# A one-row copy from ScalarE beside each group of a row softmax

## The chip, the cores and the metric

The kernel runs on one core of a Trainium2 chip. The core has five engines with an instruction stream each: TensorE (not used here), VectorE (DVE in the profile), ScalarE (ACT), GpSimd (POOL) and SyncE (SP, which issues DMA transfers). The metric is the device time of one execution in microseconds, lower is better. A profile is taken of one execution; its span runs from the first to the last instruction.

## The reference

A softmax over the last dimension of a float32 tensor with 16,384 rows of 512 elements (33.55 MB in, 33.55 MB out):

```python
batch, seq, dim = 16, 1024, 512
def reference(x):
    x_max = np.max(x, axis=-1, keepdims=True)
    exp_x = np.exp(x - x_max)
    return (exp_x / np.sum(exp_x, axis=-1, keepdims=True)).astype(np.float32)
```

## The kernel before

The 16,384 rows are cut into 16 groups. A group is 8 rows on each of the 128 partitions, a tile of 128 x 4096 float32 (2 MB). All tiles lie in `ring`, a buffer in on-chip memory with room for 12 groups; a group is worked on in place.

Transfers move two groups at a time, 4 MB: loads L0 to L7 (line 127) and stores S0 to S7 (line 131). Both are issued by SyncE, in a fixed order. The first six loads fill the ring at the start, the very first ahead of the opening barrier. After that SyncE follows `ORDER`, written out by hand: S0 S1 L6 L7 S2 S3 S4 S5 S6 S7. Before a store it waits until both groups are scaled (line 170), before L6 and L7 until S0 and S1 have landed, since these loads reuse the ring (line 197). At the end it waits for all stores (line 199).

Per group, three steps:

1. Row maxima, negated, on VectorE (`rowmax`, line 145), for one group ("M") or two ("MM") in an instruction. It waits for the load and counts up the semaphore `maxima`.
2. Exponentials on ScalarE (`exps`, lines 149 to 155): a hardware loop over the 16 groups. Each turn waits for `maxima`, computes the group's place in the ring, and issues 8 activations (line 134), one for each of the partition's rows, 128 x 512, with the negated maximum as bias and the row's sum accumulated into `stat`. The eighth counts up `summed`.
3. Scaling (`scale`, lines 157 to 163): VectorE waits for `summed`, takes the reciprocal of the 8 sums (line 159), and then VectorE ("D") or GpSimd ("P") multiplies the group by it (line 161) and counts up the semaphore that the store waits for.

VectorE's order is written out in `SEQUENCE`: M0 M1 M2 D0 M3 D1 MM4 P2 MM6 D3 P4 MM8 D5 P6 MM10 D7 P8 MM12 D9 P10 MM14 D11 P12 D13 D14 D15. It does its instructions strictly in that order, so a reciprocal that waits for ScalarE also holds up the row maxima behind it. ScalarE issues no transfers.

Of the kernel before, what the change touches and what calls it, by code (L numbers as in the profile page):

```python
# [15 lines left out]
GROUP = 8  # L16
# [44 lines left out]
def kernel(  # L61
# [5 lines left out]
    nc = tc.nc  # L67
# [3 lines left out]
    x_rows, out_rows = x.flatten_outer_dims(), out.flatten_outer_dims()  # L71
# [11 lines left out]
    def sem(name):  # L83
        return ctx.enter_context(nc.semaphore(name))

    maxima, summed, inverted = [sem(s) for s in ("maxima", "summed", "inverted")]
    loaded = [sem(f"loaded{k}") for k in range(len(LOADS))]
    scaled = [sem(f"scaled{k}") for k in range(len(STORES))]

# [43 lines left out]
    def exp(row, one):  # L133
        return nc.scalar.activation(  # L134
            out=row, in_=row, func=EXP, bias=one, scale=1.0, accum_out=one
        )
# [5 lines left out]
    def rowmax(g, groups):  # L142
# [3 lines left out]
            out=cols(stat, g, groups), in_=rows(g, groups), axis=AX, negate=True  # L146
        ).then_inc(maxima, groups)

    def exps():
        with nc.Fori(0, GROUPS, 1, engines=(ACT,)) as g:  # L150
            nc.scalar.wait_ge(maxima, 1).then_inc(maxima, -1)  # L151
            row = nc.scalar.snap((g % RING) * GROUP)
            for r in range(GROUP):
                done = exp(ring[:, bass.ds((row + r) * d, d)], stat[:, bass.ds(row + r, 1)])
            done.then_inc(summed, 1)

# [23 lines left out]

    nc.scalar.preload_act_table(EXP)  # L181
    exps()
    for work in SEQUENCE.split():
        kind = work.rstrip("0123456789")
# [46 lines left out]
```

## Time and profile before

| what | value |
|---|---|
| time, median of 3 runs | 159.97 us (159.87 to 160.02) |
| the profiled execution | 160.08 us, of which span 158.8 us |
| DVE busy | 121.8 us (77%) |
| ACT busy | 92.2 us (58%) |
| POOL busy | 42.3 us (27%) |
| line 134, an activation of 128 x 512 | 707 ns, 128 of them |
| line 145, row maxima of one group / of two | 4415 ns / 8650 ns |
| line 161, multiply on DVE / on POOL | 5109 ns / 7016 ns |
| transfers | 8 loads and 8 stores of 4096 KB |
| issue to landing, median | loads 25.9 us, stores 24.0 us |

Busy time counts an engine's work, not its waits, nor the issuing of transfers. "DMA share" is the part of the time in which the core's 16 DMA engines have packets under way. A transfer is told by its issue on the queue of the issuing engine (SPq for SyncE) and by its landing, the moment its semaphore is complete. In a list by time the columns are start, duration, engine, line, operation, output and input, and in brackets the idle time before it and what ended that. In the rows of an issue the three numbers of ns are the shortest, median and longest duration of the issuing instruction, then come the first and the last start in us.

### The profile page before, as it was taken

The page shows a single profiled execution, that of the slowest core. Times are in us where ns is not written, and L with a number is a line of the kernel's source. Part 1 is how long each engine was busy: PE and PEld are TensorE (multiplying, and loading weights), DVE is VectorE, ACT ScalarE, POOL GpSimd, SP SyncE. Part 2 cuts the span into 40 slices and gives each one's busy share as a digit, 9 for nine tenths or more (in the row PEclk, how much of TensorE's full clock was granted, in tenths as well). Part 3 has the DMA queues.
Part 4 walks back from the last instruction along what each step waited for, and adds up shares of the span by engine and source line. Part 5 has one row for each costly group of instructions (what it writes and reads, how often), then busy time and mean ns, then how long its engine had stood idle before and what let it go on. Part 6 is the DMA issues. An engine that isn't in the chain of part 4 may idle for free.

```text
span 158.8 us, 572 instructions
## 1 busy us (share of the span) xinstructions
DVE 121.8 (77%) x36; ACT 92.2 (58%) x257; POOL 42.3 (27%) x10
## 2 busy tenths in 40 slices
DVE  0008979999999999999999499999999999700000
ACT  0300699969406999999988990899599300000000
POOL 0000000000007903930970790079049300000000
DMA  7999999999999999999999999999999999999996
GB/s 264 438 479 405 405 495 421 396 438 471 413 405 438 471 405 396 396 413 471 438 396 462 446 413 405 454 421 438 438 421 446 413 446 438 438 421 438 429 429 264
DMA packets 2304, 67.11 MB, mean 423 GB/s; under 512 B 256, under 2 KB 256, under 8 KB 256
## 3 DMA queue, kind: packets, MB, share of 16 engines
q1 hardware_dynamic: 2304, 67.11, 98.9%
HBM read 33.55 MB, written 33.55 MB: 423 GB/s over the span
## 4 chain that ended last, share of the span: by engine, by line
DMA 45%; DVE 39%; issue 2%; DVEq 0%
DMA ring<-in_x_dram 26%; DVE ring L161 22%; DMA out_dram<-ring 20%; DVE stat L145 16%; DVE recip L159 1%; DVEq L144 0%
## 5 line engine op out<-in xcount | busy, mean ns | idle before, releaser
L134 ACT ACTIVATE ring<-ring,stat x128 | 90.4, 707 | 28.1 <-ACTq L151 28.1
L145 DVE TENSOR_REDUCE stat<-ring 128x16 f32<-128x8192 f32 (+1 forms) x10 | 69.5, 6956 | 15.7 <-DMA ring<-in_x_dram 15.7
L161 POOL TENSOR_TENSOR ring<-ring,recip 128x4096 f32<-128x4096 f32 x6 | 42.1, 7016 | 81.8 <-DVE recip L159 81.8
L161 DVE TENSOR_TENSOR ring<-ring,recip 128x4096 f32<-128x4096 f32 x10 | 51.1, 5109 | 0.3
L134 ACT ACTIVATION_READ_ACCUMULATOR ring<-ring,stat x128 | 23.8, 186 | 0.0
L181 ACT ACT_TABLE_LOAD x1 | 1.3, 1283 | 4.0 <-PEq L179 4.0
L159 DVE RECIPROCAL recip<-stat 128x8 f32<-128x8 f32 x16 | 3.0, 190 | 0.0
L215 POOL MEMSET const-float32-0.0<- 128x1 f32 x1 | 0.1, 98 | 0.2 <-issue 0.2
L215 POOL MEMSET const-bfloat16-1.0<- 128x1 bf16 x1 | 0.1, 102 | 0.0
L215 POOL MEMSET const-uint8-127<- 128x1 uint8 x1 | 0.1, 102 | 0.0
L215 POOL MEMSET const-float32-1.0<- 128x1 f32 x1 | 0.1, 98 | 0.0
## 6 DMA issues: line engine op xcount, KB each, us to landing
ring<-in_x_dram SPq DMA_DIRECT2D x8, 4096.0 KB, 25.9
out_dram<-ring SPq DMA_DIRECT2D x8, 4096.0 KB, 24.0
```

Of the source, the lines that this page charges most:

```text
L134: return nc.scalar.activation(out=row, in_=row, func=EXP, bias=one, scale=1.0, accum_out=one)
L145: nc.vector.reduce_max(out=cols(stat, g, groups), in_=rows(g, groups), axis=AX, negate=True).then_inc(maxima, groups)
L159: nc.vector.reciprocal(out=cols(recip, g), in_=cols(stat, g)).then_inc(inverted, 1)
L161: engine.tensor_mul(out=rows(g), in0=rows(g), in1=spread(cols(recip, g))).then_inc(scaled[store_of(g)], 1)
L181: nc.scalar.preload_act_table(EXP)
L215: nc = _bacc.Bacc("TRN2", target_bir_lowering=False, num_devices=1)
```

## The change

At the start of every turn of ScalarE's loop, after the wait for `maxima`, ScalarE issues a transfer of its own: row 0 of `x` (512 float32, 2 KB) is copied in main memory to the last row of the output. Ahead of the eighth activation of the turn ScalarE waits until the copy has landed, and takes the semaphore back to zero. The last store, S7, writes the same output row after all copies have landed, since it waits for group 15, whose eighth activation waits for the last copy.

```diff
     maxima, summed, inverted = [sem(s) for s in ("maxima", "summed", "inverted")]
+    copied = sem("copied")
...
     def exps():
         with nc.Fori(0, GROUPS, 1, engines=(ACT,)) as g:
             nc.scalar.wait_ge(maxima, 1).then_inc(maxima, -1)
             row = nc.scalar.snap((g % RING) * GROUP)
+            nc.scalar.dma_start(out=out_rows[-1:, :], in_=x_rows[:1, :]).then_inc(copied, 16)
             for r in range(GROUP):
+                if r == GROUP - 1:
+                    nc.scalar.wait_ge(copied, 16).then_inc(copied, -16)
                 done = exp(ring[:, bass.ds((row + r) * d, d)], stat[:, bass.ds(row + r, 1)])
             done.then_inc(summed, 1)
```

## The prediction

> **What bounds the kernel now.** I read the page's counts of DMA first, then the chain of waits, then the DMA issues one by one, then the order of time on ScalarE and VectorE. The page says:
>
> ```profile
> span 158.8 us, 572 instructions
> DMA  7999999999999999999999999999999999999996
> DMA packets 2304, 67.11 MB, mean 423 GB/s; under 512 B 256, under 2 KB 256, under 8 KB 256
> q1 hardware_dynamic: 2304, 67.11, 98.9%
> DMA 45%; DVE 39%; issue 2%; DVEq 0%
> ```
>
> One queue, q1, carries everything, and its packets fill 98.9% of sixteen engines' span. 256 packets are small (16 transfers on 16 engines: their completions), the other 2048 carry 67.11 MB, 32 KB each. The chain's share of 39% for DVE is no bound: it runs through VectorE because a store was issued there, but stores queue. The issues show this; for the first loads, the last of the six early loads (the largest number of its line), and stores S0, S6 and S7:
>
> ```profile
> L127 SPq DMA_DIRECT2D ring<-in_x_dram x2: 333/358/383, 0.0 to 0.8; - x2
> DMA to landing us min/median/max: 12.3/16.8/21.2
> ...
> L127 SPq DMA_DIRECT2D ring<-in_x_dram x3: 444/473/524, 1.6 to 2.7; - x3
> DMA to landing us min/median/max: 39.8/49.0/58.6
> ...
> L131 SPq DMA_DIRECT2D out_dram<-ring x1: 347/347/347, 40.0 to 40.0; - x1
> DMA to landing us min/median/max: 31.1/31.1/31.1
> ...
> L131 SPq DMA_DIRECT2D out_dram<-ring x1: 332/332/332, 128.7 to 128.7; - x1
> DMA to landing us min/median/max: 20.4/20.4/20.4
> ...
> L131 SPq DMA_DIRECT2D out_dram<-ring x1: 332/332/332, 137.8 to 137.8; - x1
> DMA to landing us min/median/max: 20.9/20.9/20.9
> ```
>
> The first load lands at 12.3 us, the last store at 137.8 + 20.9 = 158.7. That is 15 more transfers in 146.4 us, 9.76 us each. S6 lands at 128.7 + 20.4 = 149.1, S7 9.6 later: S7 was issued 11.3 us before its turn came. The first load took 12.3 - 9.76 = 2.5 us beyond its own moving time, so S7 had 11.3 - 2.5 = 8.8 us to spare. S0 was issued at 40.0 while loads were queued until 2.7 + 58.6 = 61.3. The bound is therefore the DMA stream, and computation has slack. How much ScalarE has, its first group shows:
>
> ```profile
> 17.14 0.72 ACT L134 ACTIVATE ring<-ring,stat  x1 [11.89 <-ACTq L151]
> ...
> 22.08 0.71 ACT L134 ACTIVATE ring<-ring,stat  x1
> 22.70 0.19 ACT L134 ACTIVATION_READ_ACCUMULATOR ring<-ring,stat  x1
> ...
> 26.39 0.19 DVE L159 RECIPROCAL recip<-stat 128x8 f32<-128x8 f32 x1
> ```
>
> Rows follow each other by (22.08 - 17.14)/7 = 0.706 us; the group is summed at about 22.9, and VectorE, still in its row maxima, takes the reciprocal at 26.4: 3.5 us to spare. In the table of waits ScalarE stands idle for 28.1 us in six waits for maxima.
>
> **The change, part by part.** Nothing is removed or moved. Added are 16 issues on ScalarE's sequencer, 16 transfers of 2 KB from memory to memory on a queue of ScalarE's own, and 16 waits ahead of each group's last exp.
>
> *The issue.* The nearest row is SyncE's own issue, 332 to 524 ns. At 0.34 us, 16 make 5.4 us on ScalarE's sequencer. In back-to-back groups it lies beside the exp still running; at a fresh start it delays the group by 0.34 us. The hiding work is VectorE's row maxima (3.5 us in group 0) and the 28.1 us of idle time. Taken at 0; without that cover, 5.4.
>
> *The wait.* Let L be the time from a copy's issue to its semaphore. Hidden are the issue (0.34) and seven rows (4.94), 5.3 us. No row shows a small transfer. Bounds: 2.5 us, the first load's time beyond its moving; and 58.6 us, the longest any transfer stood in q1. Between them: a 32 KB packet takes 9.76/8 = 1.22 us, since each engine has 8 of a transfer's 128. If an engine takes the two queues in turns, the copy's data wait for at most one such packet and its completion for another: 2.5 + 2 x 1.22 = 4.9 us. I take 4.9, for the copy stands on another queue than the 58.6, and 4.9 is under 5.3: nothing added. Behind the waiting instruction stand the group's last exp with its count in `summed`, the next wait for maxima and the next copy; VectorE's reciprocal (line 159) waits for the count, behind it VectorE's later row maxima, GpSimd's multiplies, then SyncE's store.
>
> When does it decide? The period of a group on ScalarE becomes L + 0.3 (the loop's own sequencer steps, an estimate from rows of 17, 35 and 74 ns and the branch) where that exceeds 5.65. The last count comes at 16.8 + 16 periods + 0.9, then reciprocal and multiply (0.2 + 4.4), then 12.3 for a store with nothing ahead. That reaches 158.7 at a period of 7.8, L = 7.5. Until there the wait costs nothing in the end, because S7's 8.8 us take it; above, every further us of L costs 16.
>
> The Trainium skill, page "DMA: Bandwidth & Descriptors", section "Queues, rings and completion order", states that an engine goes round its queues packet by packet, and that SyncE and ScalarE own one queue each. By that the sum has no term for the wait; by the order inside q1, the only one this trace shows, it would be the third rival below.
>
> *The DMA time.* This is not hidden: copies go out between 16.8 and about 120 us, all inside a stream without gaps, and what an engine spends on a copy pushes back all behind it. Lower bound: 2 KB spread over 16 engines is 128 B each, 1.22 us x 128/32768 = 0.005 us a copy, 0.08 us for 16. If a single engine carries the row, 1.22 x 2/32 = 0.076 us a copy, 1.2 us for 16, and the slowest engine decides. A turn from one queue to the other is not shown. The nearest rows are the steps between landings inside q1: the last early load lands at 61.3, S0 at 71.1, 9.8 us for a change from loads to stores, against a mean of 9.76; the longest step is the next, 10.0 to S1 (61.8 + 19.3 = 81.1). So a turn costs up to about 0.3 us and may cost nothing: 16 x 0.3 = 4.8 us at the upper end. A gain is hard to see: the stream has no gap that a second queue could fill. I take 0.06 us a copy, nearer the small end, because the 256 small completions already in the stream leave it 98.9% full; one turn of 0.3 in five copies or a row on one engine would make about that. 16 x 0.06 = 0.96 us.
>
> The same page, section "Specifications", puts line rate at 512 B and more and says that the engine reads and rewrites below it. Counting my 0.06 twice for this gives 1.9 us, 161.9 in all, an estimate from that rule; no run here shows it yet.
>
> *Sum.* The profiled execution took 160.08 us, 158.8 of span and 1.28 around it. 160.08 + 0 + 0 + 0.96 = 161.0. It was 0.11 above the median of 159.97, so against the runs shown I forecast 160.9.
>
> **Rivals.** *First, the copies vanish in the stream (the other side, not slower).* Place: sixteen engines with packets of 128 B. Price 0.08 us, total 160.05. It holds while a copy takes under 0.32/16 = 0.02 us of an engine. For it: the completions in the stream cost nothing that I can see. Against it: one engine, or one exposed turn in 15, is enough to leave it.
>
> *Second, turns are dear:* each copy costs the full 0.3 us, 4.8 us, 164.8. For it: the 10.0 us between S0 and S1, just behind the first change of direction. Against it: the next step, a change back to loads, is short (L6 lands at 71.1 + 19.5 = 90.6, 9.5 us later), so the 10.0 may be an uneven landing.
>
> *Third, the copy lands late and ScalarE becomes the bound.* With L = 8 the end is 16.8 + 16 x 8.3 + 0.9 + 4.6 + 12.3 + 1.3 = 168.7. It decides from L = 7.5, for example if five 32 KB packets in all go ahead of the copy's two small ones (2.5 + 5 x 1.22 = 8.6), or if a copy stands behind queued transfers as S0 did (31.1). With a whole transfer ahead, L = 2.5 + 9.76 = 12.3, the end is 16.8 + 16 x 12.6 + 0.9 + 4.6 + 12.3 + 1.3 = 237.5, less in fact, since engines then run dry and L falls. For it: every wait for a landing in this trace is above 12 us. Against it: those are 4 MB each, in one queue.
>
> *Fourth, faster:* only if a second queue kept engines busy over a start or an end. All that is not packets is 1.1% of 158.8, 1.7 us, nearly all before the first packet, where no copy is out yet.
>
> **How the numbers follow.** Forecast, slower by 0.3 to 3 us: 0.47. Copies vanish: 0.20. Dear turns: 0.09. Late copies: 0.19. Faster: 0.05. A measurement of this kernel can tell about 0.2% (0.32 us) from no change. Slower is the forecast with the second and third rival, 0.75; same 0.20; faster 0.05. The forecast alone ranges from 160.3 to 163. The range for 8 in 10 has to hold the vanishing copies and the dear turns and the near part of late copies: 159.8 to 168. It leaves out most late copies and nearly all of the faster case.
>
> **What would show it.** A second DMA queue with 16 copies, and small packets added. Right: ScalarE's idle time before the last exp of a group close to 0, copies landing within about 5.3 us, DMA still at 9 in every slice, transfers each landing 9.8 to 9.9 us apart while copies go out and 9.76 or less after them. Wrong on L: ScalarE idle seven rows into each group, with landings over 7.5 us and slices of DMA under 9 near the end. Wrong on the DMA time: the store landings spread by more than 0.3 us a transfer, or not at all.

## The result, and the profile after

The changed kernel takes 160.38 us in the median of 17 runs (160.03 to 160.61), the kernel before 159.95 (159.75 to 161.02). The ratio is 1.0025, with a 95% interval of 1.0016 to 1.0033: slower by 0.40 us (0.26 to 0.53). The forecast was 0.95 us slower. The profiled execution took 160.31 us, 159.0 of it span.

From the page of the changed kernel, its span, the DMA counts and the row of the new transfers (kind, number, KB each, median us from issue to landing):

```profile
span 159.0 us, 604 instructions
DMA packets 2816, 67.14 MB, mean 422 GB/s; under 512 B 768, under 2 KB 768, under 8 KB 768
q1 hardware_dynamic: 2304, 67.11, 98.7%
q10 hardware_dynamic: 512, 0.03, 0.2%
out_dram<-in_x_dram ACTq DMA_DIRECT2D x16, 2.0 KB, 7.0
```

The copies run on a second queue, q10, with 512 packets: 16 copies x 16 engines x 2, one of data (128 B) and one for the completion. They fill 0.2% of the engines' span, 0.32 us, while q1 carries what it did before. The packet records in the trace, which the page only sums up, give it without the rounding: a data packet of 128 B takes 13 ns and a completion 9 ns, so a copy takes 22 ns on each engine and 16 copies take 0.35 us. A copy lands after 7.0 us, not after the 4.9 of the prediction.

So ScalarE does wait. From the tables of waits (who waited for what: us in total, times, longest), first one line of the kernel before, where line 151 is the wait for maxima, then three of the changed kernel (line 158 is the wait for the copy, line 153 the one for maxima, line 164 the reciprocal):

```profile
ACT ring L134 <- ACTq L151: 28.1, 6, 11.9
...
ACT ring L135 <- ACTq L158: 19.7, 14, 2.0
ACT ring L135 <- ACTq L153: 15.1, 2, 12.6
DVE recip L164 <- ACT ring L135: 11.9, 3, 6.9
```

In 14 of 16 groups ScalarE stands 1.4 us on average for the copy. Nearly half of its idle time for maxima (28.1 us before, 15.1 now) is used up by this, and VectorE now waits 11.9 us for ScalarE, which it did nowhere before. Among the last stores S6 is hardly later (issued at 129.0 against 128.7 before), S7 is. Their DMA issues, one by one:

```profile
L132 SPq DMA_DIRECT2D out_dram<-ring x1: 332/332/332, 129.0 to 129.0; - x1
DMA to landing us min/median/max: 20.3/20.3/20.3
...
L132 SPq DMA_DIRECT2D out_dram<-ring x1: 332/332/332, 143.3 to 143.3; - x1
DMA to landing us min/median/max: 15.7/15.7/15.7
```

S7 is issued 5.5 us later than before (143.3 against 137.8) and still lands 9.7 us after S6 (159.0 against 149.3), as any store in an unbroken stream. It had 6.0 us left before its turn. The lateness does not reach the end; what reaches it is 0.3 us by which the whole stream is longer.

### The profile page after: what moved, and what is told of

It reads as the page before. It is cut to its first block, busy times and chain, and to the rows that moved or that the text cites. A ratio compares the mean times of both kernels' runs of the same rounds, so it can differ in the third digit from the quotient of the medians.

```text
span 159.0 us, 604 instructions
## 1 busy us (share of the span) xinstructions
DVE 115.3 (73%) x36; ACT 95.0 (60%) x257; POOL 42.3 (27%) x10
## 5 line engine op out<-in xcount | busy, mean ns | idle before, releaser
L135 ACT ACTIVATE ring<-ring,stat x128 | 90.8, 710 | 39.6 <-ACTq L158 19.7
L166 DVE TENSOR_TENSOR ring<-ring,recip 128x4096 f32<-128x4096 f32 x10 | 44.2, 4425 | 0.3
L164 DVE RECIPROCAL recip<-stat 128x8 f32<-128x8 f32 x16 | 3.1, 195 | 11.9 <-ACT ring L135 11.9
```

Source lines behind the costliest of these rows:

```text
L135: return nc.scalar.activation(out=row, in_=row, func=EXP, bias=one, scale=1.0, accum_out=one)
L164: nc.vector.reciprocal(out=cols(recip, g), in_=cols(stat, g)).then_inc(inverted, 1)
L166: engine.tensor_mul(out=rows(g), in0=rows(g), in1=spread(cols(recip, g))).then_inc(scaled[store_of(g)], 1)
```

## The experiments

Two explanations of the 0.40 us were tried against each other: A, the copies' packets take time on the DMA engines; B, the lateness of ScalarE and of the last stores. Times in this section are ratios to the kernel before, run on the same chip, times its median there.

**The changed kernel again.** 

> The changed kernel itself, on the chip on which the three others of this group run. Both theories: 0.3 to 0.5 us above the kernel before, on this chip too.

Measured: ratio 1.0018 (1.0003 to 1.0033), 0.29 us (0.05 to 0.53), with q10 at 0.2% again. A repeat by itself tells A from B no better.

**Late, without copies.**

```diff
-            nc.scalar.dma_start(out=out_rows[-1:, :], in_=x_rows[:1, :]).then_inc(copied, 16)
...
-                    nc.scalar.wait_ge(copied, 16).then_inc(copied, -16)
+                    for k in range(2):
+                        nc.scalar.activation(
+                            out=idle[:, k * d : (k + 1) * d], in_=zeros[:, :],
+                            func=EXP, bias=zeros[:, :1], scale=1.0,
+                            accum_out=idle_sum[:, k : k + 1],
+                        ).then_inc(copied, 1)
+                    nc.scalar.wait_ge(copied, 2).then_inc(copied, -2)
```

`zeros` is filled once at the start.

> No copy is issued. In its place ScalarE computes two unused exponentials of 128 x 512 ahead of the eighth row of each group and waits for them, so that each group takes about 7.3 us instead of 5.65, as with the copies. Theory A (the copies' packets take time on the DMA engines: 512 packets, 0.2% of the span): no copies, no cost, within 0.1 us of the kernel before. Theory B (the lateness of ScalarE and of the last stores costs the 0.4 us): 0.3 to 0.5 us above the kernel before, as with the copies.

Measured: ratio 1.0002 (0.9989 to 1.0015), 0.03 us (-0.18 to 0.24). The issues of its last two stores, S6 and S7, together:

```profile
L136 SPq DMA_DIRECT2D out_dram<-ring x2: 332/332/332, 128.8 to 142.5; - x2
DMA to landing us min/median/max: 16.0/18.1/20.1
```

S7 goes out at 142.5, nearly as late as in the changed kernel, and lands 16.0 later at 158.5. The same lateness without the packets costs nothing that can be measured, so B falls: on this chip the median of the twelve runs is 160.11 us, for the changed kernel 160.31, for the kernel before 160.03.

**The copies, covered.** A turn of the loop takes two groups:

```diff
-        with nc.Fori(0, GROUPS, 1, engines=(ACT,)) as g:
+        with nc.Fori(0, GROUPS // 2, 1, engines=(ACT,)) as h:
             nc.scalar.wait_ge(maxima, 1).then_inc(maxima, -1)
...
+            for c in range(2):
+                last = out_rows.shape[0] - 1 - c
+                nc.scalar.dma_start(
+                    out=out_rows[last : last + 1, :], in_=x_rows[:1, :]
+                ).then_inc(copied, 16)
+            for r in range(2 * GROUP):
+                if r == GROUP:
+                    nc.scalar.wait_ge(maxima, 1).then_inc(maxima, -1)
+                if r == 2 * GROUP - 1:
+                    nc.scalar.wait_ge(copied, 32).then_inc(copied, -32)
...
```

> The same 16 copies, two at the start of every second group (to the last and the last but one row), awaited ahead of the sixteenth row, so 15 rows (10.6 us) lie over a landing of 7 us and ScalarE hardly waits for it; stores are issued as early as in the kernel before. Theory A: the same 512 packets, 0.3 to 0.5 us above the kernel before. Theory B: within 0.1 us of the kernel before.

Measured: ratio 1.0019 (1.0004 to 1.0033), 0.30 us (0.06 to 0.53). ScalarE waits for copies once, for 0.2 us, and S7 goes out at 138.2, against 137.8 before. With the lateness gone the cost is still there (a median of 160.37 us).

**Twice the copies.** The same with `range(4)` and 64 in place of 32. 

> As the covered version, but four copies at the start of every second group: 32 copies, 1024 small packets. Theory A: twice the cost, 0.6 to 1.0 us above the kernel before. Theory B: the four issues (0.5 us each) make ScalarE about 2 us later in every second group, less than the changed kernel's waits: under 0.3 us.

Measured: ratio 1.0044 (1.0027 to 1.0061), 0.70 us (0.43 to 0.98). The page:

```profile
q10 hardware_dynamic: 1024, 0.07, 0.4%
```

0.4% of 159.4 us is 0.64 us.

**Sixteen rows a copy.** `out_rows[-16:, :]` and `x_rows[:16, :]` in the copy. 

> Each copy takes 16 rows (32 KB) in place of one, so a data packet is 2 KB in place of 128 B if all sixteen engines share it; the number of copies, packets and waits is the same. By the rate of the big packets (32 KB in 1.22 us) the added 1.9 KB take 0.07 us on an engine, 16 x 0.07 = 1.1 us more than the changed kernel, so about 1.5 us above the kernel before, if bytes set the price. If the price is one of turns between queues, whatever their size: 0.4 us above the kernel before.

Measured: ratio 1.0097 (1.0075 to 1.0120), 1.55 us (1.20 to 1.92). The page:

```profile
q10 hardware_dynamic: 512, 0.53, 0.9%
out_dram<-in_x_dram ACTq DMA_DIRECT2D x16, 32.0 KB, 6.8
```

The number of packets, the landing and ScalarE's waits are those of the changed kernel; only the bytes grew. 0.9% of 160.8 us is 1.45 us. For all three amounts of copies the cost is the share of q10 times the span and little else: 0.32, 0.64 and 1.45 us against 0.40, 0.70 and 1.55. By the packet records, without the rounding of the shares, it is 0.35, 0.70 and 1.49 us (a data packet of 2 KB takes 84 ns). No price of a turn between queues is left to find that exceeds the intervals.

**Smaller big packets.** Loads and stores with a cap on the piece, 8 KB here and 16 KB in the second kernel; the copies stay. What was expected of the 16 KB version stands first below; its "the same" refers to the 8 KB version behind it.

```diff
-        return nc.sync.dma_start(out=rows(g, n), in_=in_dram(x_rows, g, n))
+        return nc.sync.dma_start(out=rows(g, n), in_=in_dram(x_rows, g, n), max_dma_last_dim=8192)
...
-        return nc.sync.dma_start(out=in_dram(out_rows, g, n), in_=rows(g, n))
+        return nc.sync.dma_start(out=in_dram(out_rows, g, n), in_=rows(g, n), max_dma_last_dim=8192)
```

> The same with pieces of 16 KB, 0.61 us each. Theory Q: landings of 2.5 + 3.7 x 0.61 = 4.8 us. Theory M: near 7 us.

> Copies as in the changed kernel, but the loads and stores are cut into pieces of 8 KB in place of 32 KB, so a big packet takes 0.31 us in place of 1.22. Theory Q (a copy's landing is the 2.5 us of a lone transfer and turns behind some 3.7 big packets): landings fall from 7.0 to about 3.6 us and ScalarE's waits for the copies vanish. Theory M (the landing is the memory's own answer under load): landings stay near 7 us. The total also has the cost of four times the packets, in either theory.

Measured with 16 KB: 160.55 us, ratio 1.0036 (1.0024 to 1.0048), landings of 5.9 us in the median. With 8 KB: 170.46 us, ratio 1.066, landings of 5.2. On the two pages, 16 KB first:

```profile
out_dram<-in_x_dram ACTq DMA_DIRECT2D x16, 2.0 KB, 5.9
...
out_dram<-in_x_dram ACTq DMA_DIRECT2D x16, 2.0 KB, 5.2
```

Neither theory named these: the landing follows the size of the big packets, but less steeply than Q said. From 7.0 to 5.9 to 5.2 us while the packet falls from 1.22 to 0.61 to 0.31 us, that is (7.0 - 5.2)/(1.22 - 0.31) = 2.0 packets, and what remains is 7.0 - 2 x 1.22 = 4.6, 5.9 - 1.22 = 4.7 and 5.2 - 0.6 = 4.6 us. This fits two big packets ahead of a copy, one for each of its own two, as the prediction had it; the rest is 4.6 us, not 2.5. The packet records show both packets directly. Between a copy's data packet and its completion on the same engine lie 1.22, 0.62 and 0.32 us in the median, one big packet of each version. And from the first of the sixteen engines to start its data packet to the last, 1.5, 0.9 and 0.6 us pass, where a copy without a stream beside it has 0.2.

The 8 KB version also shows a copy with idle DMA engines, in a hole of the stream between 72 and 78 us. Its time by stretches (us of the stretch, busy time and instructions of DVE, ACT and POOL, PE clock, DMA share, GB/s):

```profile
72.00:78.00 6.00, 5.97 (x5) 6.00 (x19) 0.32 (x1) 1.00 0.00 0
```

And its copies one by one, first two at the hole, then two well ahead of it:

```profile
L155 ACTq DMA_DIRECT2D out_dram<-in_x_dram x2: 517/517/517, 69.9 to 73.0; - x2
DMA to landing us min/median/max: 1.9/2.0/2.2
...
L155 ACTq DMA_DIRECT2D out_dram<-in_x_dram x2: 517/517/517, 44.9 to 51.2; - x2
DMA to landing us min/median/max: 4.9/4.9/4.9
```

With the DMA share at 0, a copy lands in 1.9 us; under the stream it takes 4.9. Its total time says nothing about the copies: SyncE's six first load issues take 28.3 us in place of 3.17, the activation table is loaded after 29.1 us instead of 4.0, the first group starts at 33.7 us instead of 17.0, and the engines run dry.

**The copies alone.** The loop holds only the copy and its wait. 

> Only the sixteen copies, one after the other, each awaited; loads, stores and all computation are left out, so the output is not the softmax. Theory Q2 (a landing is 1.9 us of its own, about two big packets of turns, and some 2.8 us more that only a busy stream adds): landings of 1.9 to 2.2 us here, as in the hole of the 8 KB version. Theory F (the 4.7 us that remain without the turns are the copy's own, fixed): landings near 4.7 us.

Measured: a span of 36.5 us, and on the page

```profile
out_dram<-in_x_dram ACTq DMA_DIRECT2D x16, 2.0 KB, 1.8
```

A lone copy lands in 1.8 us, as in the hole. The 4.6 us are therefore 1.8 of its own and 2.8 that only a busy stream adds. The packet records place nearly all of these 2.8 us ahead of the copy's first packet. Alone, a copy's first data packet starts 1.30 us after the issue; under the stream it starts after 4.0 us in the changed kernel, 3.9 with pieces of 16 KB and 3.8 with 8 KB (medians). From the last completion packet to the semaphore it is 0.34 us alone and 0.39 in the changed kernel. What a copy waits for in these first 4 us, the records don't say.

**The copy into on-chip memory.** `out=spare[:1, :]`, a row of one partition, in place of the output's last row. 

> The changed kernel with the copy's destination in on-chip memory (a spare row of one partition) in place of the output's last row. If the extra 2.8 us under load is the write to main memory and its answer: landings fall from 7.0 to about 4.2 us. If it is the way to the engines or the read: they stay at 6.5 to 7.2 us. The packets, and with them the cost of some 0.4 us, stay in either case (one execution can't tell that).

Measured: a single execution of 161.46 us, against 160.04 for the kernel before. The expectation was off at its last sentence: the packets do not stay. This copy makes 32 packets in place of 512, so one engine carries all 2 KB. ScalarE's waits for the copy fall from 19.7 to 3.4 us, so landings are shorter:

```profile
ACT ring L136 <- ACTq L159: 3.4, 9, 1.0
```

That has two possible reasons, the target and the single engine (no slowest of sixteen to wait for). The packet records speak for the second: the data packet starts 3.9 us after the issue, as the first of the sixteen does in the changed kernel (4.0), and the completion packet after 5.1 us, again as the first of the sixteen (5.1), while the last of the sixteen starts its completion after 6.6. So the wait ahead of the first packet is about as long with either target, and what is gone is the slowest engine of sixteen. (Its issue also takes 0.21 us instead of 0.52, so the two are not alike in all.) The same kernel again, timed in six executions:

> The copy to a spare row in on-chip memory, timed. Its profile showed 32 packets on the copies' queue in place of 512: one data packet of 2 KB and one completion a copy, so one engine carries all of it. By the 32 KB packets' rate 16 x 1.22 x 2/32 = 1.2 us on that engine, and more for the completions: if the slowest engine sets the end, 1.2 to 1.6 us above the kernel before. If the sum over all engines counted (0.1% of the span), under 0.2 us.

Measured: 161.90 us, ratio 1.0125 (1.0106 to 1.0145), 2.0 us (1.7 to 2.3). Its page says

```profile
q10 hardware_dynamic: 32, 0.03, 0.1%
```

and its last stretch, with the columns as above, where the changed kernel has a DMA share of 0.00 and 0 GB/s:

```profile
158.00:161.00 3.00, 0.00 (x0) 0.00 (x0) 0.00 (x0) 1.00 0.03 11
```

11 GB/s over 3 us are 33 KB, a single packet of 32 KB: by the packet records one engine starts its last packet at 158.98 us and ends it at 160.2, while the other fifteen are done by 158.6. It still works off what the copies pushed back. Smaller in the mean over the engines (0.1% against 0.2%), the copy costs five times as much. Its two packets take 84 + 9 = 93 ns, 1.49 us for 16, the same as on every engine of the sixteen-row copies, which cost 1.55. The 2.0 us are above that and above the 1.2 to 1.6 expected; where the rest (0.2 to 0.8 us) goes is open.

**A later issue.** The copy goes out ahead of the third row instead of the first:

```diff
-            nc.scalar.dma_start(out=out_rows[-1:, :], in_=x_rows[:1, :]).then_inc(copied, 16)
             for r in range(GROUP):
+                if r == 2:
+                    nc.scalar.dma_start(out=out_rows[-1:, :], in_=x_rows[:1, :]).then_inc(copied, 16)
                 if r == GROUP - 1:
```

> The copy is issued ahead of the third row of each group instead of the first, the wait stays ahead of the eighth, so two rows (1.4 us) of cover are lost. Theory S (the waits of the changed kernel are paid from S7's spare time, of which 6.0 - 2.5 = 3.5 us are left, and beyond that every us a group costs 16): a period of 7.54 + 1.4 = 8.95 us, last sum 16 x 1.4 = 22 us later than 138.4 less the 2.5 us that ScalarE now waits for maxima, S7 issued at about 163 and landing 12.3 later, so 175 to 177 us, less if landings get shorter when the DMA engines run dry (not under 166). Theory N (a wait for a small copy costs nothing that shows in the time): 160.4.

Measured: 161.41 us in the median of eight runs that lie far apart (160.54 to 163.24), ratio 1.0074 (1.0048 to 1.0099), 1.18 us (0.77 to 1.58). The profiled execution took 162.16. Both theories miss it. In order of time around the start of one group (the first row is the eighth of the group before):

```profile
120.10 0.72 ACT L135 ACTIVATE ring<-ring,stat  x1 [1.64 <-ACTq L159]
120.82 0.70 ACT L135 ACTIVATE ring<-ring,stat  x1
120.93 0.52 ACTq L157 DMA_DIRECT2D out_dram<-in_x_dram  x1
121.52 0.71 ACT L135 ACTIVATE ring<-ring,stat  x1
122.23 0.70 ACT L135 ACTIVATE ring<-ring,stat  x1
```

The copy stands in the program behind two rows, but it is issued while the first of them runs: the sequencer hands rows to the engine and goes on. It goes out 0.83 us after the eighth row starts; in the changed kernel that is 0.40 (116.26 against 115.86). So 0.43 us a group are lost, not 1.4, and the period goes from (130.4 - 17.0)/15 = 7.56 to (137.3 - 17.4)/15 = 7.99 us. The issue of S7:

```profile
L132 SPq DMA_DIRECT2D out_dram<-ring x1: 332/332/332, 149.7 to 149.7; - x1
DMA to landing us min/median/max: 11.1/11.1/11.1
```

S7 is 6.4 us later than in the changed kernel and lands at 160.8 instead of 159.0. A store with nothing ahead lands 11.1 us after its issue, a store in the stream 9.7 us after the one before it, so the 6.0 us that S7 had left were 6.0 - 1.4 = 4.6 to spare, and 6.4 - 4.6 = 1.8 us reach the end. That this is the difference of the two landings follows from the way it is reckoned; what the trace adds is that S6 had landed at 133.9 + 15.4 = 149.3, before S7 was issued, so that S7 had nothing ahead.

## Why the prediction was wrong

**The bound** was right: the DMA stream, with computation behind it.

**The DMA time** was the right term with the wrong size, and it is where the forecast failed: "I take 0.06 us a copy", 0.96 us in all. Measured: 0.40/16 = 0.025 us. The prediction's lower figure of 0.005 counted the bytes alone; q10's packets take 0.022 a copy on each engine (13 ns for the data, 9 ns for the completion). I went up from there for two things that did not happen. A row carried by one engine: the copy to main memory is spread over all sixteen (512 packets); the run where one engine does carry it shows that case at 2.0 us. And an exposed turn of up to 0.3 us, read from the uneven landings of S0 and S1: with twice the copies and with sixteen rows a copy the cost stays at the packets' own time (0.70 and 1.49 us of packets against 0.70 and 1.55 measured). The reading of q1's 256 completions, which leave it 98.9% full, pointed to that and should have been taken at its word.

**The wait** was priced at nothing, rightly, but for half the reason. The two packets ahead of a copy were right (2.0 measured). "The first load's time beyond its moving", 2.5 us, was the wrong row for the rest: 4.6 under the stream. L was therefore 7.0, above the 5.3 us of cover and 0.5 short of the 7.5 at which I saw the third rival begin. The cover of seven rows hid 5.3 us of it. What hid the rest was ScalarE's idle time for maxima, which fell from 28.1 to 15.1 us, and then S7's spare time, which fell from 11.3 to 6.0 us before its turn. A period of ScalarE was 7.56 us, 0.56 above L and not 0.3, so the edge at a period of 7.8 was only 0.24 us a group away. The formula for the edge held in kind: lateness is free until the spare time is used up, then counts in full, as the later issue shows; its spare time was 1.1 us too small, since a store alone lands in 11.1 us and not in 12.3 like the first load. With the later issue's period of 7.99 us and the store's 11.1, the formula gives 16.8 + 16 x 7.99 + 0.9 + 4.6 + 11.1 = 161.2 us; S7 landed at 160.8.

**The issue** took 0.52 us, not 0.34, and shows as 4.6 us of idle time on ScalarE, hidden as the rest.

**The rivals.** The vanishing copies were the nearest in size. The interval of 0.26 to 0.53 excludes their price of 0.08 us, but the limit that the prediction gave them, 0.32 us in all, lies inside it: the measured 0.40 is nearer to this rival than to the forecast of 0.95. Dear turns, 4.8 us, fall by all three amounts of copies. Late copies came close and did not decide. Faster: no sign.

**The two rules of the Trainium skill**, page "DMA: Bandwidth & Descriptors". Section "Queues, rings and completion order", the turns between queues: the runs agree, a copy waits for two packets and not for the transfers queued in q1, where S0 stood 31.3 us. Section "Specifications", the rewriting below 512 B: the 1.9 us that I worked out from it is not seen; copies of 128 B a packet cost 0.40 us. Packets of 128 B, 2 KB and 32 KB took 13, 84 and 1213 ns (median), about 8.5 ns and their bytes at one rate, with no further time below 512 B.

## What to carry to other kernels

When the DMA engines are full, a small extra transfer costs about its own packets' time on the busiest engine (0.35, 0.70 and 1.49 us of packets cost 0.40, 0.70 and 1.55 here; on a single engine 1.49 cost 2.0), so look first at how many engines share it, then at its bytes. Its wait is another matter: price a landing under load from a landing under load, not from the first transfer on idle engines, and compare it with the spare time of the last transfer, which hid several microseconds here and none after that. When a profile shows a growing wait and the same time, look at how much earlier than its turn the last store is issued: that is what is left.

## What the runs showed of the hardware that I had not expected

A 2 KB copy lands in 1.8 us alone and in 7.0 us beside a full stream of 32 KB packets; 2.4 us of that are the two packets ahead, and 2.8 us come from the stream whatever its packet size (32, 16 or 8 KB). These 2.8 us pass almost entirely before the copy's first packet starts (4.0 us after the issue instead of 1.30), and the wait is about as long when the copy goes to on-chip memory (3.9), so a target in main memory is not what it is for. What causes it was not settled.

Cutting the loads into 8 KB pieces made SyncE's first six load issues take 28.3 us in place of 3.17, and 16 KB pieces 8.84; I had taken the time of an issue for a constant. It is not the number of pieces in one issue alone that counts: with 8 KB the first three issues took at most 0.51 us and the next three 7.3, 9.5 and 9.6; with 16 KB only the sixth was long, 5.9 us; and the stores, issued later and with as many pieces, took 0.37 to 0.47 us in both. An issue was long where several loads of many pieces had been issued just before it.

VectorE's multiply took 4425 ns in the mean, against 5109 before: the one of 11.27 us, which ran beside GpSimd's last, is gone because ScalarE's lateness moved them apart (the mean is 4535 ns with the lateness and no copies, and 5110 with the copies covered). Busy time fell by 6.5 us for a kernel that got slower. It is also why S7 is only 5.5 us later although VectorE waited 11.9 us: the multiply gave back 11.27 - 4.42 = 6.85 us.
